# Inverting the 32x32 diagonal blocks of a gated delta rule as two 16x16 halves per block

## The chip, the cores and the metric

The kernel runs on one core of one Trainium2 chip. The metric is device time in microseconds for one execution. Three runs of the kernel before gave 2830.55, 2837.04 and 2839.18 us, so the median is 2837.04 us.

## The reference, cut to what matters

The kernel is one block of a hybrid model: a modulated norm, a mixer that has an RG-LRU branch and a gated delta-rule branch (8 heads of 128, two directions), an output projection, and a feed-forward part with squared ReLU. The data is 512 latent tokens and 256 context tokens, everything in float32. The change touches the delta rule alone, which works in chunks and solves one unit triangular system for each:

```
l_mat = jnp.einsum('bhncd,bhnsd->bhncs', k_beta, k_c) * decay
rhs = jnp.concatenate([v_beta, k_beta * jnp.exp(g_cum)[..., None]], axis=-1)
sol = lax.linalg.triangular_solve(l_mat, rhs, left_side=True, lower=True, unit_diagonal=True)
u_c, w_c = sol[..., :dv], sol[..., dv:]
qk = jnp.einsum('bhncd,bhnsd->bhncs', q_c, k_c) * decay
...
v_new = u_i - jnp.einsum('bhck,bhkv->bhcv', w_i, state)
o_i = jnp.einsum('bhck,bhkv->bhcv', q_dec_i, state) + jnp.einsum('bhcs,bhsv->bhcv', qk_i, v_new)
state = state * cd_i[..., None, None] + jnp.einsum('bhck,bhcv->bhkv', k_dec_i, v_new)
```

## The kernel before, in words

The kernel works in chunks of 128 tokens, twice the reference's. For each chunk it forms the inverse of the unit triangular 128x128 matrix explicitly, and then multiplies by it.

**Stages.** First come the modulation vectors (to about 165 us). Then `run_tiles` (L485) works through a hand-written order `ORD` (L1164) of output columns of the input projection; each tile multiplies 16 pieces of weights, split in a high and a low part, with the tokens (L498 to L500, three products each). `project` (L1334) then does the output projection, and `ff1_half`, `ff1` and `ff2` the feed-forward part. The first matrix of a weight piece is cast on ScalarE (L67), the low part is a subtraction on VectorE or GpSimd (L61). L61 and L64 are the lines of the helpers `tt` and `stt`, so that many different operations carry them; the tile names tell these apart.

**Order of the work.** Everything beside the tiles is a generator. `slot()` (L388) is called once for each piece of a tile (12 matmuls of 512 columns, or 24 of 256) and gives every generator a turn: it adds 2.8 us of VectorE and 2.2 us of ScalarE to a budget, and a generator runs on to its next `yield v, a, wait` as long as both budgets are positive; `v` and `a` are costs written by hand, and `wait` is a number of slots to stand back. `boundary()` (L430) fixes how far an instruction may be moved from the slot in which it was written: three slots on TensorE, SyncE and GpSimd, two on ScalarE, one on VectorE. So the weight matmuls of a tile and the work of the delta rule lie in one queue on each engine, in an order that is fixed when the kernel is built.

**The delta rule.** `Group.run` (L804) runs six times: two groups of context heads and four of latent heads. It builds the matrices `Ab` for both directions (L814 to L857), 16 of 128x128 in all, so that there are 64 diagonal blocks of 32x32. `Cm` (L868 to L872) collects these. Two VectorE transposes (L880) bring each block whole into two lanes (partitions) as `L`. A lane holds every second row of the inverse in the PSUM bank `Wt`, starting from the unit matrix (L885 to L888). Then 31 steps (L890 to L897), each a product (`tmp`) and a subtraction (`Wt`), finish the inverse; every fourth step ends in a `yield 1.4, 0, 0`. Two transposes (L901, L902) bring the result back as `YT` and `Yc`. The 32x32 inverses are then joined to 64x64 (products L925, L934, L937) and to 128x128 (L948 to L958), and the recurrence over the chunks follows (L977 to L1049). `afree` counts the groups that may hold `Ab` (2, later 3) and those that may hold `L` (1).

Small products in this part are given as 32x32 tiles: contraction over 32 partitions, output into 32 partitions of a PSUM bank. One of these float32 matmuls leaves two records in the trace. PSUM has 8 banks, which `bank()` hands out in turn to tiles, evacuations and the delta rule alike.

Of the kernel before, what the change touches and what calls it, by code (L numbers as in the profile page):

```python
# [7 lines left out]
F32 = mybir.dt.float32  # L8
F32R = mybir.dt.float32r
I32 = mybir.dt.int32  # L10
AF = mybir.ActivationFunctionType
ALU = mybir.AluOpType
# [4 lines left out]
P = 128  # L17
# [14 lines left out]
def build(tc, A, out, stop=None, dump=None):  # L32
    nc = tc.nc
    V, S, G, T, SP = nc.vector, nc.scalar, nc.gpsimd, nc.tensor, nc.sync
    es = ExitStack()
    with es:
        cp = es.enter_context(tc.tile_pool(name="const", bufs=1))
        wp = es.enter_context(tc.tile_pool(name="weights", bufs=2))
        pp = es.enter_context(tc.tile_pool(name="pages", bufs=29))
        ld_n = 5  # L40

        pg = ps = es.enter_context(tc.tile_pool(name="psum", bufs=8, space=PSUM))
# [3 lines left out]
        def nm(s):  # L46
            cnt[0] += 1
            return f"{s}_{cnt[0]}"

        def page(dt=F32, tag="pg", shape=(P, 512), bufs=None):  # L50
            kw = {} if bufs is None else {"bufs": bufs}
            return pp.tile(list(shape), dt, tag=tag, name=nm(tag), **kw)

        def bank(pool=None, tag="b"):
            return (pool or ps).tile([P, 512], F32, tag=tag, name=nm("bk"))

        def const(shape, dt, name):
            return cp.tile(list(shape), dt, name=name, tag=name)

        def tt(e, out, a, b, op):  # L60
            e.tensor_tensor(out=out, in0=a, in1=b, op=op)  # L61

        def stt(out, a, s, b, op0, op1):
            V.scalar_tensor_tensor(out=out, in0=a, scalar=s, in1=b, op0=op0, op1=op1)  # L64
# [7 lines left out]
        ones = const([P, P], F32, "ones")  # L72
# [33 lines left out]
        def quad(nm_, dt=F32R):  # L106
            return pp.tile([P, 4, 512], dt, tag="q8", name=nm(nm_), bufs=8)
# [31 lines left out]
        for src, n, dst in ((v1, 128, c1), (v2, 121, c2), (v3, 96, c3)):  # L139
            b = bank()  # L140
# [24 lines left out]
        def rsqrt(x, w):  # L165

            y = sm.tile([P, 16], I32, tag="rq_y", name=nm("rqy"))[:, :w]
            t = sm.tile([P, 16], F32, tag="rq_t", name=nm("rqt"))[:, :w]
            V.tensor_scalar(out=y, in0=x.bitcast(I32), scalar1=-0.5, scalar2=MAGIC, op0=ALU.mult, op1=ALU.add)
            yf = y.bitcast(F32)  # L170
            for _ in range(3):
                stt(t, yf, -0.5, yf, ALU.mult, ALU.mult)
                tt(V, t, t, x, ALU.mult)
                stt(yf, t, 1.5, yf, ALU.add, ALU.mult)
            return yf
# [56 lines left out]
        def v4(t):  # L232
            return t.rearrange("p (u i) -> p u i", i=P)

        def transp(src):
            b = bank()
            for i in range(4):
                T.transpose(b[:, i * P:(i + 1) * P], src[:, i * P:(i + 1) * P], ident)
            return b
# [31 lines left out]

        scol = const([P, 2, 16], F32, "scol")
        shc = const([P, 2, 16], F32, "shc")
        A_BUFS = 7

        def hctx(f):

            if f < 3:
                return [page(F32R, shape=(P, 2, 256)) for _ in range(2)]
            x = pp.tile([P, 4, 256], F32R, tag="A", name=nm("Hc"), bufs=A_BUFS)  # L280
            return [x[:, 0:2], x[:, 2:4]]
# [26 lines left out]
        for j, (f, kind, k0) in enumerate(mpieces):  # L308
            if k0 == 0:
                pm = bank(pg)  # L310
            r = mraw.pop(j)
            h, l = quad("mh"), quad("ml")
# [37 lines left out]
        mpar = const([P, 2], F32, "mpar")  # L350
# [32 lines left out]
        def spawn(gen, order, rate=None, prio=0):  # L383
            t = Task(gen, order, rate, prio)
            tasks.append(t)
            return t
# [27 lines left out]
        def finish(t):  # L414
            while not t.done:
                t.step()
            for l in (tasks, evacs):
                if t in l:
                    l.remove(t)
# [241 lines left out]
        def gates(n, res):  # L661
# [3 lines left out]
            def evac(pt):  # L665
# [4 lines left out]
                for t in range(NT):  # L670
                    T.transpose(b[:, t * 32:(t + 1) * 32], gf[:32, t * P:(t + 1) * P], ident[:32, :32])
                key = "L" if n == LAT else "C"
                raw = page(shape=(P, 32, NT))
# [69 lines left out]
        class Group:  # L743
# [60 lines left out]
            def run(self):  # L804
# [8 lines left out]
                afree[0] -= 1  # L813
                Ab = [pp.tile([P, 8, P], F32, tag="A", name=nm("A"), bufs=A_BUFS) for _ in range(2)]  # L814
                if lat:
                    ptD = dp.tile([2, 2, P, 512], F32, tag="ptD", name=nm("ptD"), bufs=3)
                sh4 = [P, 4, P]
                for p in range(2):
                    rr, dts = [], []
                    for d in range(2):  # L820
# [3 lines left out]
                        for u in range(4):  # L824
                            S.activation(v4(rh)[:, u, :], mk, AF.Copy, scale=gt["gh"][:, o + u:o + u + 1].bitcast(F32))
                            G.tensor_scalar(out=v4(rl)[:, u, :], in0=mk, scalar1=gt["gl"][:, o + u:o + u + 1].bitcast(F32),
                                            scalar2=0.0, op0=ALU.mult, op1=ALU.add)
# [40 lines left out]
                Cm = page(shape=(P, 16, 32))  # L868
                for b in range(4):
                    sb = slice(32 * b, 32 * b + 32)  # L870
                    S.copy(Cm[sb, 0:8], blk(Ab[0], b, 32 * b, 32))
                    V.transpose(Cm[sb, 8:16], blk(Ab[1], b, 32 * b, 32))  # L872
                yield 1.4, 1.3, 0
                while not afree[1]:
                    yield 0, 0, H0
                afree[1] -= 1
                L = pp.tile([P, 32, 32], F32, tag="A", name=nm("L"), bufs=A_BUFS)
                cv_ = Cm.rearrange("p u i -> p i u").unsqueeze(2).to_broadcast([P, 32, 2, 16])
                for i in range(2):
                    V.transpose(L[:, 16 * i:16 * i + 16].rearrange("p i (e j) -> p i e j", e=2), cv_[:, 16 * i:16 * i + 16])  # L880
                Lr = L.rearrange("p i j -> p j i")
                wf = bank()
                Wt = wf.rearrange("p (j i) -> p j i", i=32)
                tmp = page(shape=(P, 16, 32))
                V.memset(wf, 0.0)  # L885
                for e in range(2):
                    V.tensor_scalar(out=wf[:, e:512:34], in0=ones[:, 0:16], scalar1=mpar[:, e:e + 1], scalar2=0.0,
                                    op0=ALU.mult, op1=ALU.add)  # L888
                yield 1.6, 0, 0
                for l in range(31):  # L890
                    nr = l // 2 + 1
                    sh = [P, nr, 31 - l]
                    tt(V, tmp[:, :nr, l + 1:], Wt[:, :nr, l:l + 1].to_broadcast(sh), Lr[:, l:l + 1, l + 1:].to_broadcast(sh),
                       ALU.mult)
                    tt(V, Wt[:, :nr, l + 1:], Wt[:, :nr, l + 1:], tmp[:, :nr, l + 1:], ALU.subtract)
                    if l % 4 == 3:
                        yield 1.4, 0, 0  # L897
                afree[1] += 1
                Yc = page(shape=(P, 16, 32))
                YT = page(shape=(P, 16, 32))  # L900
                V.transpose(YT.rearrange("p u (r e) -> p r e u", e=2), Wt.rearrange("p r (e u) -> p r e u", e=2))  # L901
                V.transpose(Yc, YT)  # L902
                yield 1.9, 0, 0
                Ud = (Yc[:, 0:8], YT[:, 8:16])
                Dd = (YT[:, 0:8], Yc[:, 8:16])

# [15 lines left out]
                for u in range(8):  # L922
                    for d in range(2):
                        for i, j in pairs(d):
                            T.matmul(bP[sl32(j), u, :], Ab[d][sl32(i), u, sl32(j)], Dd[d][sl32(i), u, :],  # L925
                                     start=True, stop=True)
# [4 lines left out]
                for u in range(8):  # L931
                    for d in range(2):
                        for i, j in pairs(d):
                            T.matmul(bU[d][sl32(i), u, :], Pn[sl32(j), u, :], Ud[d][sl32(j), u, :],  # L934
                                     start=True, stop=True)
                            if (d, j) in ((0, 1), (1, 2)):
                                T.matmul(bU[d][sl32(j), u, :], Ud[d][sl32(j), u, :], Pn[sl32(j), u, :],  # L937
                                         start=True, stop=True)
# [38 lines left out]
                for st in range(1 if lat else 2):  # L977
                    sv = v4(Sst[h0 // 2 + st])
                    for s in range(NT):
                        ch = []  # L980
                        for d in range(2):
                            for hh in range(2):
                                p = hh if lat else st
                                t = s if d == 0 else NT - 1 - s
                                u = t if lat else hh * 2 + t
# [24 lines left out]
                        bY = v4(bank())  # L1010
# [49 lines left out]
                r = rsqrt(ss, 8)  # L1060
# [10 lines left out]
                for p in range(2):  # L1071
                    b = transp(O[p])
# [93 lines left out]
        H0, H1, H2, H3 = 1, 1, 1, 1  # L1166
        PG = (2, 2, 2, 2, 2, 2)
        PL = (-1, -1, -3, 1, -3, -1, -1, -1)
        PU, PO, NA, FILL = -1, (-1, -2, 1), 3, 0.0
        afree = [2, 1]  # L1170

        def T_(col, n, ev, m=P):
            return dict(col=col, m=m, n=n, hl=hl_lat if n == LAT else hl_ctx, evac=ev)
# [6 lines left out]
        def mods(chunks, after=None):  # L1180
            for ch in chunks:
                for f in range(4):
                    yield from modacc(ch, f, after)
# [3 lines left out]
        def set_rate(r):  # L1187
            if modtask:
                modtask[0].rate = r or None
# [4 lines left out]
        def set_lru(n):  # L1194
            LRU_MAX[0] = n
# [8 lines left out]
            "F": [lambda: finish(lh)], "m": [lambda: modtask.append(spawn(mods((2, 3, 4)), 3, MOD_RATE or None, PO[1]))],  # L1204
            "L": [lambda: set_lru(2)],
            "1": [lambda: set_rate(0)], "2": [lambda: set_rate(0.6)],
# [13 lines left out]
        for d in seq:  # L1220
            if not callable(d):
                e = (V, G) if d["n"] == CTX else (G, G)
# [20 lines left out]
        def big4(i):  # L1243
            if i < 3:
                xs = [pp.tile([P, 1024], F32, tag="A", name=nm("big"), bufs=A_BUFS) for _ in range(2)]
                return [xs[c // 2][:, c % 2 * 512:c % 2 * 512 + 512] for c in range(4)]
# [254 lines left out]
        b = NB - 1  # L1501
        wl_ = []
        for c in range(4):
            h8, l8 = quad("w2h"), quad("w2l")
            for k0 in range(0, 4, 2):
                r = wp.tile([P, 1024], F32, tag="wr", name=nm("wr"), bufs=3)
# [38 lines left out]
```

## Time and profile before

| what | value |
|---|---|
| median of three runs | 2837.04 us |
| profiled execution, its own time | 2838.08 us |
| its span, first to last instruction | 2836.3 us |
| mean granted TensorE clock | 0.970 |
| the six inversions, first transpose of `L` to last transpose back (start of L880 to end of L902) | 296.2 to 328.2, 476.1 to 539.1, 640.2 to 685.5, 758.4 to 823.9, 1049.2 to 1098.9, 1150.5 to 1194.4 us |

In the page and the views of the profile, PE is TensorE, PEld its weight loads, DVE VectorE, ACT ScalarE, POOL GpSimd. Rows of groups end in the busy time, the mean length of one in ns, and the engine's idle time just before them with what ended it. Rows of waits give total us, times, and the longest. Rows of stretches give from:to, length, the busy time of each engine with its number of instructions, and then the granted clock, the share of time in which the DMA engines were busy, and GB/s.

### The profile page before, as it was taken

The page shows a single profiled execution, that of the slowest core. Times are in us where ns is not written, and L with a number is a line of the kernel's source. Part 1 is how long each engine was busy: PE and PEld are TensorE (multiplying, and loading weights), DVE is VectorE, ACT ScalarE, POOL GpSimd, SP SyncE. Part 2 cuts the span into 40 slices and gives each one's busy share as a digit, 9 for nine tenths or more (in the row PEclk, how much of TensorE's full clock was granted, in tenths as well). Part 3 has the DMA queues.
Part 4 walks back from the last instruction along what each step waited for, and adds up shares of the span by engine and source line. Part 5 has one row for each costly group of instructions (what it writes and reads, how often), then busy time and mean ns, then how long its engine had stood idle before and what let it go on. Part 6 is the DMA issues. An engine that isn't in the chain of part 4 may idle for free.

```text
span 2836.3 us, 39412 instructions
## 1 busy us (share of the span) xinstructions
PE 2652.2 (94%) x14189; PEld 2187.4 (77%) x14189; DVE 1694.6 (60%) x3286; ACT 1193.2 (42%) x2374; POOL 639.1 (23%) x580
## 2 busy tenths in 40 slices
PE   5788899899999998977999999999999999999998
PEld 1278797788777887766898887888888888888886
DVE  6787757777696777836598533443434444334436
ACT  4546466654556564535553222222222222222222
POOL 3545344344344353315410000000000000000002
PEclk8899999999999998988999999999999999999999
DMA  7854465466566666746678433333333333333335
GB/s 269 269 141 140 109 179 170 145 188 192 172 178 194 190 199 210 223 153 202 203 259 280 160 99 115 97 97 97 97 97 97 97 97 98 96 99 97 98 98 155
DMA packets 376629, 436.39 MB, mean 154 GB/s; under 512 B 22793, under 2 KB 213602, under 8 KB 376434
## 3 DMA queue, kind: packets, MB, share of 16 engines
q1 hardware_dynamic: 376434, 433.89, 49.2%
q8 instruction: 111, 1.82, 0.3%
q14 instruction: 84, 0.69, 0.1%
HBM read 402.35 MB, written 31.46 MB: 153 GB/s over the span
## 4 chain that ended last, share of the span: by engine, by line
PE 57%; DVE 3%; DMA 2%; issue 1%; POOL 1%; ACT 1%; SPq 0%; DVEq 0%; ACTq 0%; POOLq 0%
PE bk L1461 8%; PE bk L1459 8%; PE bk L1460 8%; PE bk L1448 7%; PE bk L1450 7%; PE bk L1449 7%; PE bk L1370 2%; PE bk L1371 2%; PE bk L1369 2%; PE bk L1420 1%; PE bk L1419 1%; PE bk L1418 1%; DVE pg L61 1%; DMA wr<-in_w_ff 1%; PE bk L498 1%
## 5 line engine op out<-in xcount | busy, mean ns | idle before, releaser
L67 ACT CAST wh<-wr 128x512 fp32r<-128x512 f32 x952 | 584.6, 618 | 1226.9 <-PE bk L1449 446.1
L61 DVE TENSOR_TENSOR wl<-wr,wh 128x512 fp32r<-128x512 f32 x642 | 462.9, 723 | 785.8 <-ACT wh L67 664.6
L61 POOL TENSOR_TENSOR wl<-wr,wh 128x512 fp32r<-128x512 f32 (+1 forms) x310 | 403.8, 1308 | 594.5 <-ACT wh L67 537.2
L1461 PE MATMUL bk<-wl,pg 128*128 128x512 f32 x960 | 373.7, 389 | 0.0
L1459 PE MATMUL bk<-wh,pg 128*128 128x512 f32 x960 | 373.7, 389 | 0.0
L1460 PE MATMUL bk<-wh,pg 128*128 128x512 f32 x960 | 373.6, 389 | 0.0
L1448 PE MATMUL bk<-H2h,wh 128*128 128x512 f32 x896 | 350.0, 391 | 0.0
L1449 PE MATMUL bk<-H2l,wh 128*128 128x512 f32 x896 | 349.2, 390 | 0.0
L1450 PE MATMUL bk<-H2h,wl 128*128 128x512 f32 x896 | 349.2, 390 | 0.0
L498 PE MATMUL bk<-Hlh,wh 128*128 128x512 f32 (+1 forms) x784 | 318.5, 406 | 0.0
L500 PE MATMUL bk<-Hlh,wl 128*128 128x512 f32 (+1 forms) x784 | 311.5, 397 | 1.8 <-POOL wl L61 1.8
L499 PE MATMUL bk<-Hll,wh 128*128 128x512 f32 (+1 forms) x784 | 311.8, 398 | 0.0
L61 POOL TENSOR_TENSOR big<-big,pg 128x512 f32<-128x512 f32 x9 | 12.2, 1369 | 1248.0 <-ACT pg L1521 1248.0
L1461 PEld LDWEIGHTS bk<-wl,pg 128*128 128x128 f32 x960 | 180.3, 188 | 37.6 <-DVE wl L61 0.4
L1460 PEld LDWEIGHTS bk<-wh,pg 128*128 128x128 f32 x960 | 180.3, 188 | 37.4
L1459 PEld LDWEIGHTS bk<-wh,pg 128*128 128x128 f32 x960 | 180.3, 188 | 37.2
L1449 PEld LDWEIGHTS bk<-H2l,wh 128*128 128x128 f32 x896 | 168.7, 188 | 35.4 <-issue 0.4
L1448 PEld LDWEIGHTS bk<-H2h,wh 128*128 128x128 f32 x896 | 168.5, 188 | 35.1 <-issue 0.2
L1450 PEld LDWEIGHTS bk<-H2h,wl 128*128 128x128 f32 x896 | 168.6, 188 | 35.0
L500 PEld LDWEIGHTS bk<-Hlh,wl 128*128 128x128 f32 (+1 forms) x784 | 149.5, 191 | 36.2 <-POOL wl L61 2.3
L498 PEld LDWEIGHTS bk<-Hlh,wh 128*128 128x128 f32 (+1 forms) x784 | 150.0, 191 | 31.0 <-ACT pg L1045 0.2
L499 PEld LDWEIGHTS bk<-Hll,wh 128*128 128x128 f32 (+1 forms) x784 | 150.0, 191 | 30.4
(336 smaller groups left out, 4577.8 us busy)
## 6 DMA issues: line engine op xcount, KB each, us to landing
wr<-in_w_ff SPq DMA_DIRECT2D x272, 512.0 KB
wr<-in_w_in SPq DMA_DIRECT2D x144, 512.0 KB
ld<-in_w_mod SPq DMA_DIRECT2D x256, 256.0 KB
mr<-in_w_mod SPq DMA_DIRECT2D x32, 1024.0 KB
wr<-in_w_out SPq DMA_DIRECT2D x64, 512.0 KB
pg<-vkD SPq DMA_DIRECT2D x88, 128.0 KB
ld<-in_x SPq DMA_DIRECT2D x32, 256.0 KB
vkD<-pg SPq DMA_DIRECT2D x24, 256.0 KB
```

The lines of the kernel that those rows point to most:

```text
L61: e.tensor_tensor(out=out, in0=a, in1=b, op=op)
L67: S.copy(hi, src)
L498: T.matmul(pt[:m, :n], wh, a, start=k == 0, stop=False)
L499: T.matmul(pt[:m, :n], wh, b, start=False, stop=False)
L500: T.matmul(pt[:m, :n], wl, a, start=False, stop=k == 15)
L1369: T.matmul(bk[t], mh[:, s_], h, start=st, stop=False)
L1448: T.matmul(bk[c], w[kk][0][:, s_], hh, start=k == 0, stop=False)
L1449: T.matmul(bk[c], w[kk][0][:, s_], hl_, start=False, stop=False)
L1450: T.matmul(bk[c], w[kk][1][:, s_], hh, start=False, stop=k == 15)
L1459: T.matmul(o, ah, h, start=k == 0, stop=False)
L1460: T.matmul(o, al, h, start=False, stop=False)
L1461: T.matmul(o, ah, l, start=False, stop=k == 3)
```

## The change

Each 32x32 block is split into its two 16x16 diagonal halves and the 16x16 quarter off the diagonal. A lane now holds one half (`mpar` is 1 in the lanes of one half and 0 in the others, and picks which), so that the 64 blocks still fill 128 lanes. 15 steps invert the halves. The halves go back, as a 32x32 matrix `Y0` with an empty quarter (and its transpose `YT0`), and the quarter follows from two products for each block: Z = -(N times YT0), with N the quarter (`Nm`), and then Z with Y0, once for the inverse and once for its transpose. `YT0` is laid out so that the first product can take N as it stands.

By engine, for each of the six groups: VectorE loses 32 of 62 step instructions, one transpose, and one of two diagonal writes, and its bank memset is half as wide; it gains one multiply-add over 256 columns and two additions over 512. ScalarE gains five copies (two over 256 columns from SBUF, two over 256 from PSUM, one over 512 from PSUM). GpSimd gains a memset. TensorE gains 64 and then 128 matmuls of 32x32x32. Three more banks are taken in turn. `L` is now an ordinary page, so that the count for it in `afree` falls away; there are 31 pages instead of 29, and 6 buffers of the tag "A" instead of 7. The costs in the `yield`s, from `Lx` to the point where the 64x64 join starts, were 13.3 us of VectorE (1.6, seven times 1.4, 1.9) and are 11.4 us of VectorE (1.8, three times 2.1, 1.9, 1.4) and 2.5 us of ScalarE, with one wait of a slot (`H1`) before the first product and none between the first and the second product.

```diff
-        pp = es.enter_context(tc.tile_pool(name="pages", bufs=29))
+        pp = es.enter_context(tc.tile_pool(name="pages", bufs=31))
...
-        A_BUFS = 7
+        A_BUFS = 6
...
-                while not afree[1]:
-                    yield 0, 0, H0
-                afree[1] -= 1
-                L = pp.tile([P, 32, 32], F32, tag="A", name=nm("L"), bufs=A_BUFS)
-                cv_ = Cm.rearrange("p u i -> p i u").unsqueeze(2).to_broadcast([P, 32, 2, 16])
-                for i in range(2):
-                    V.transpose(L[:, 16 * i:16 * i + 16].rearrange("p i (e j) -> p i e j", e=2), cv_[:, 16 * i:16 * i + 16])
+
+                Lx = page(shape=(P, 16, 32))
+                V.transpose(Lx.rearrange("p i (e j) -> p i e j", e=2), Cm.rearrange("p u (e i) -> p i e u", e=2))
+                L = page(shape=(P, 16, 16))
+                S.activation(L, Lx[:, :, 0:16], AF.Copy, scale=mpar[:, 0:1])
+                stt(L, Lx[:, :, 16:32], mpar[:, 1:2], L, ALU.mult, ALU.add)
+                Nm = page(shape=(P, 16, 32))
+                G.memset(Nm, 0.0)
+                S.activation(Nm[:, :, 16:32], Cm[:, :, 16:32], AF.Copy, scale=mpar[:, 0:1])
                 Lr = L.rearrange("p i j -> p j i")
-                wf = bank()
-                Wt = wf.rearrange("p (j i) -> p j i", i=32)
-                tmp = page(shape=(P, 16, 32))
+                wf = bank()[:, 0:256]
+                Wt = wf.rearrange("p (j i) -> p j i", i=16)
+                tmp = page(shape=(P, 16, 16))
                 V.memset(wf, 0.0)
-                for e in range(2):
-                    V.tensor_scalar(out=wf[:, e:512:34], in0=ones[:, 0:16], scalar1=mpar[:, e:e + 1], scalar2=0.0,
-                                    op0=ALU.mult, op1=ALU.add)
-                yield 1.6, 0, 0
-                for l in range(31):
-                    nr = l // 2 + 1
-                    sh = [P, nr, 31 - l]
-                    tt(V, tmp[:, :nr, l + 1:], Wt[:, :nr, l:l + 1].to_broadcast(sh), Lr[:, l:l + 1, l + 1:].to_broadcast(sh),
-                       ALU.mult)
-                    tt(V, Wt[:, :nr, l + 1:], Wt[:, :nr, l + 1:], tmp[:, :nr, l + 1:], ALU.subtract)
-                    if l % 4 == 3:
-                        yield 1.4, 0, 0
-                afree[1] += 1
-                Yc = page(shape=(P, 16, 32))
-                YT = page(shape=(P, 16, 32))
-                V.transpose(YT.rearrange("p u (r e) -> p r e u", e=2), Wt.rearrange("p r (e u) -> p r e u", e=2))
-                V.transpose(Yc, YT)
-                yield 1.9, 0, 0
+                V.tensor_copy(wf[:, 0:256:17], ones[:, 0:16])
+                yield 1.8, 0.9, 0
+                for l in range(15):
+                    sh = [P, l + 1, 15 - l]
+                    tt(V, tmp[:, :l + 1, l + 1:], Wt[:, :l + 1, l:l + 1].to_broadcast(sh),
+                       Lr[:, l:l + 1, l + 1:].to_broadcast(sh), ALU.mult)
+                    tt(V, Wt[:, :l + 1, l + 1:], Wt[:, :l + 1, l + 1:], tmp[:, :l + 1, l + 1:], ALU.subtract)
+                    if l % 5 == 4:
+                        yield 2.1, 0, 0
+                We = page(shape=(P, 16, 32))
+                for e in range(2):
+                    S.activation(We[:, :, 16 * e:16 * e + 16], Wt, AF.Copy, scale=mpar[:, e:e + 1])
+                Y0 = page(shape=(P, 16, 32))
+                YT0 = page(shape=(P, 16, 32))
+                V.transpose(YT0.rearrange("p u (e r) -> p r e u", e=2), We.rearrange("p r (e u) -> p r e u", e=2))
+                V.transpose(Y0, YT0)
+                del We, wf, Wt, tmp, L, Lr, Lx
+                yield 1.9, 0.9, H1
+                bZ = bank().rearrange("p (u i) -> p u i", i=32)
+                for u in range(16):
+                    for b in range(4):
+                        sb = slice(32 * b, 32 * b + 32)
+                        T.matmul(bZ[sb, u, :], Nm[sb, u, :], YT0[sb, u, :], start=True, stop=True)
+                Z = page(shape=(P, 16, 32))
+                S.activation(Z, bZ, AF.Copy, scale=-1.0)
+                yield 0, 0.7, 0
+                bY = [bank().rearrange("p (u i) -> p u i", i=32) for _ in range(2)]
+                for u in range(16):
+                    for b in range(4):
+                        sb = slice(32 * b, 32 * b + 32)
+                        T.matmul(bY[0][sb, u, :], Z[sb, u, :], Y0[sb, u, :], start=True, stop=True)
+                        T.matmul(bY[1][sb, u, :], Y0[sb, u, :], Z[sb, u, :], start=True, stop=True)
+                Yc, YT = Y0, YT0
+                tt(V, Yc, Yc, bY[0], ALU.add)
+                tt(V, YT, YT, bY[1], ALU.add)
+                del Nm, Z, bZ, bY, Y0, YT0
+                yield 1.4, 0, 0
...
-        afree = [2, 1]
+        afree = [2]
```

## The prediction

> **What bounds the kernel now.** I read the page first, then busy times by stage, then the same for the stretches in which an inversion runs, then what TensorE waited for, then the groups of instructions that the change touches.
>
> ```profile
> PE 2652.2 (94%) x14189; PEld 2187.4 (77%) x14189; DVE 1694.6 (60%) x3286; ACT 1193.2 (42%) x2374; POOL 639.1 (23%) x580
> ```
>
> TensorE is busy for 94% of the span, and VectorE is next. The delta rule and the tiles that it shares the queues with lie between 165 and 1268 us:
>
> ```profile
> 165.00:1130.00 965.00, 892.78 (x5796) 763.31 (x5797) 712.97 (x1538) 550.53 (x1219) 422.69 (x408) 0.96 0.59 174
> 1130.00:1268.00 138.00, 115.72 (x853) 97.69 (x854) 90.24 (x260) 59.95 (x156) 36.11 (x29) 0.93 0.62 193
> ```
>
> In these 1103 us TensorE is idle for 72.2 + 22.3 = 94.5 us. Only this idle time can be won, and any matmul that is added there is paid in full unless it falls into it. Now the six stretches around the inversions, with their sum:
>
> ```profile
> 291.00:336.00 45.00, 37.15 (x379) 28.78 (x377) 39.70 (x107) 19.35 (x43) 14.87 (x15) 0.95 0.43 112
> 468.00:550.00 82.00, 65.82 (x352) 53.99 (x351) 65.25 (x152) 46.19 (x102) 31.09 (x27) 0.92 0.49 142
> 640.00:687.00 47.00, 44.81 (x288) 37.76 (x287) 41.43 (x113) 20.30 (x54) 17.14 (x14) 1.00 0.64 197
> 755.00:861.00 106.00, 95.43 (x535) 79.93 (x534) 97.27 (x216) 53.49 (x127) 41.16 (x35) 0.98 0.58 170
> 1049.00:1104.00 55.00, 45.62 (x256) 37.12 (x255) 47.48 (x112) 26.20 (x45) 22.43 (x18) 0.91 0.71 218
> 1150.00:1202.00 52.00, 49.24 (x329) 40.80 (x328) 47.23 (x145) 27.12 (x69) 17.63 (x14) 1.00 0.69 218
> sum 387.00, PE 338.07 PEld 278.38 DVE 338.37 ACT 192.66 POOL 144.31; mean PE 56.34 PEld 46.40 DVE 56.40 ACT 32.11 POOL 24.05
> ```
>
> Here VectorE is busy for 338.4 of 387 us, 87%, and TensorE idle for 48.9 us, 12.6%. In the other 716 us VectorE has 713.0 + 90.2 - 338.4 = 464.8 us of work, 65%, and TensorE stands for 45.6 us, 6.4%. The granted clock costs something too: time by lost share is 45 x 0.05 + 82 x 0.08 + 106 x 0.02 + 55 x 0.09 = 15.9 us, and it is lowest where the waits are longest. What TensorE waited for from 165 to 1268:
>
> ```profile
> PE bk L238 <- DVE pg L64: 18.3, 6, 5.6
> PE bk L925 <- DVE pg L901: 12.0, 4, 9.4
> PE bk L238 <- DVE pg L61: 11.0, 3, 6.3
> ```
>
> The long waits end on VectorE: transposes of evacuated tiles (L238), and the first product behind an inversion (L925), with one wait of 9.4. So in these stretches TensorE and VectorE are nearly level, and VectorE's queue is what holds TensorE up.
>
> **The change, part by part: VectorE.** The steps of before and the operations to compare with:
>
> ```profile
> L61 DVE TENSOR_TENSOR pg<-bk,L 128x126 f32<-128x126 f32 (+22 forms) x186 | 58.8, 316 | 4.5
> L61 DVE TENSOR_TENSOR bk<-bk,pg 128x126 f32<-128x126 f32 (+22 forms) x186 | 48.4, 260 | 5.0
> ```
>
> ```profile
> L61 DVE TENSOR_TENSOR pg<-bk,rqy 128x512 f32<-128x512 f32 x20 | 13.3, 684 | 0.2
> ...
> L880 DVE STREAM_TRANSPOSE L<-pg 128x512 f32<-128x512 f32 x12 | 12.8, 1094 | 0.0
> ...
> L64 DVE SCALAR_TENSOR_TENSOR pg<-bk,c,pg 128x254 f32<-128x254 f32 x24 | 11.4, 474 | 11.1 <-ACT pg L530 7.4 <-ACT pg L773 3.7
> ...
> L61 DVE TENSOR_TENSOR pg<-bk,L 128x56 f32<-128x56 f32 x12 | 3.0, 250 | 0.3
> ...
> L885 DVE MEMSET bk<- 128x512 f32 x6 | 2.9, 485 | 6.0 <-ACT pg L733 5.5
> ...
> L61 DVE TENSOR_TENSOR bk<-bk,pg 128x56 f32<-128x56 f32 x12 | 2.7, 224 | 0.3
> ...
> L61 DVE TENSOR_TENSOR bk<-bk,pg 128x16 f32<-128x16 f32 x6 | 1.1, 186 | 0.2
> L61 DVE TENSOR_TENSOR pg<-bk,L 128x16 f32<-128x16 f32 x6 | 1.1, 185 | 0.2
> ```
>
> A group has 31 steps now, 31 x (316 + 260) ns = 17.9 us. The new step l works on (l+1) x (15-l) elements, 680 over 15 steps, 45 on average. Between the rows of 16 and 56 elements a product of 45 takes 233 ns and a subtraction 214, so 15 steps take 6.7 us (5.6 if all were of 16 elements, 7.1 if all of 56). The steps save 11.2 us. Beside them two transposes of 1.094, a memset of 0.485 and two diagonal writes (16 elements, priced as a step of 16, 0.19) go, 3.1 us; a transpose of 1.09, a multiply-add of 0.47, half a memset (0.24 to 0.49), one diagonal write and two additions of 0.68 come, 3.4 us. The two transposes back stay. Net 10.8 us per group, 65 us over six.
>
> That work leaves the stretches: (338.4 - 65)/387 is 71% busy. Against it stand two new hand-overs to ScalarE and back (`L` behind `Lx`, the transposes behind `We`). No row shows these; they lie between nothing, if other VectorE work is put between, and some 2 us, above which they would be longer than most of VectorE's waits for ScalarE. The mean of the nearest row, 46.0/30 = 1.5 us, gives 18 us in six groups, so that VectorE would be taken for 75%:
>
> ```profile
> DVE wl L61 <- ACT wh L67: 46.0, 30, 4.2
> ```
>
> That is nearer to the 65% of the rest than to 87%, so I take it that TensorE's idle share falls to the rest's 6.4%: 387 x 0.064 = 24.8 us, a gain of 24.1 us. Linear between the two pairs (65% with 6.4%, 87% with 12.6%) it would be 9.2%, a gain of 13; if nothing but hand-overs were left, all of 48.9. Half of the 15.9 us of clock goes with it, 8 us (0 to 15.9).
>
> **TensorE.** 64 + 128 matmuls of 32x32x32 in each group, 1152 in all:
>
> ```profile
> L925 PE MATMUL bk<-pg,A 32*32 32x32 f32 x384 | 6.2, 202 | 13.1 <-DVE pg L901 12.0 <-DVE pg L902 1.0
> L937 PE MATMUL bk<-pg,pg 32*32 32x32 f32 x192 | 6.2, 205 | 0.0
> L934 PE MATMUL bk<-pg,pg 32*32 32x32 f32 x384 | 6.2, 204 | 0.6 <-ACT pg L928 0.6
> ```
>
> A single one takes about 0.2 us, but they overlap. L934 and L937 run interleaved in the same 6.2 us: 576 records, 288 matmuls, 21.5 ns each. L925 has 192 matmuls in 6.2 us, 32 ns each, in bursts that waits have cut. So 1152 cost 24.8 to 37 us. I take 24.8, since the new loops are as dense as L934 and L937. They stand in TensorE's queue among weight matmuls that have no slack of their own, so that nothing hides them.
>
> The Trainium skill, page "TensorEngine Tiling (Array Packing)", section "Gotcha 1: PSUM Pressure", speaks against this: tiles that differ in their rows are to write to different PSUM banks and cannot use one at the same time. In the new loops all four write to one bank. By it they would run one after another (the price is with the rivals). This trace doesn't agree: L925 writes one bank from four row tiles too, and 60 of its records end within 0.72 us:
>
> ```profile
> 328.59 0.72 PE L925 MATMUL bk<-pg,A 32*32 32x32 f32 x60
> ...
> 331.13 0.21 PE L934 MATMUL bk<-pg,pg 32*32 32x32 f32 x1 [0.55 <-ACT pg L928]
> ```
>
> **The new waits.** The chain is now transposes, Z, its evacuation on ScalarE, Y, two additions on VectorE, L925. Z comes a slot or more behind the transposes and should find them done. Between Z and Y there is no wait written, so they follow each other in TensorE's queue, unless weight matmuls are moved between. The rows above show such a hand-over: 1.8 us from the last L925 (329.3) by way of L928 to L934 (331.1), with 0.55 us of it idle, since weight matmuls ran between. So 0.1 us (0.6 over six) to 1.8 us for each group, and never below nothing, as a wait gives no time back; I take 1.0, 6 us in all. Behind a TensorE that stands there, queue the weight matmuls of the next tile, and behind those ScalarE's casts that wait for free weight buffers. The wait of L925 for the transposes turns into one for the additions; it stays within the idle share above.
>
> ScalarE gains, by the rows of L928 (256 columns) and L951 (512), 4 x 0.39 + 0.60 = 2.2 us per group, 13 us on an engine that is 50% busy in the stretches:
>
> ```profile
> L951 ACT ACTIVATE pg<-bk 128x512 f32<-128x512 f32 x6 | 3.6, 595 | 3.2 <-PE bk L949 3.2
> ...
> L928 ACT ACTIVATE pg<-bk 128x256 f32<-128x256 f32 x6 | 2.3, 386 | 0.1
> ```
>
> Hidden by that slack, as is GpSimd's memset; without it they would lengthen the hand-overs counted above. The written costs fall by 1.9 us of VectorE per group, two thirds of a slot, and the new `H1` gives it back, so I move nothing at the end of the last group. The counter for `L` never held a group up, as the inversions don't overlap. Pages, "A" buffers and the three banks I cost at nothing: pages are added, and the banks turn over in a few us each. If a bank came late, TensorE would wait as it does for an evacuation, and I leave that in the range.
>
> **The sum.** 24.8 (matmuls) + 6 (Z to Y) - 24.1 (idle) - 8 (clock) = -1.3 us, against the profiled execution's 2838.1 (1.8 above its span, 1.0 above the median of the runs): 2837. The bounds of the parts added up in full reach from -40 to +35; the forecast's own part of them is about 2823 to 2854, since idle time and clock go together and the dense price of the matmuls is the nearest row.
>
> **The rivals.**
> - *VectorE was the bound, and its relief is worth all of it.* The idle time in the stretches goes entirely, and the clock returns to 1.00: -48.9 - 15.9 + 24.8 + 6 = -34, 2804; halfway to it, 2820. For it speaks that nearly all long waits name VectorE; against it, that TensorE stands for 6.4% outside the stretches too.
> - *The hand-overs take the place of the waits* (slower). Z, Y and L925 stand behind one another, and TensorE waits 1.8 us for Z's evacuation and 2 us for the two additions (2 x 0.68 and the way there and back) in each group. It decides when less than those 1.8 us of weight matmuls come between. +24.8 + 22.8 - 32.1 = +15.5, 2854; with the idle time won back only by the linear rule (13 + 4), +30.6, 2869. For it: L925 follows L901 today with nothing written between, and waited 13.1 us in all. Against: L934 behind L928 waited 0.6 us in all.
> - *The small matmuls don't overlap* and take 0.204 us each: 1152 x 0.204 = 235 in place of 24.8, about 3047. The change then wouldn't do what it says. L925 and L934 speak against it. That is also the Trainium skill's rule above.
>
> **How the numbers follow.** 0.3% of this kernel, 8.5 us, is about what a measurement can tell from no change. Forecast 0.52, of which 0.12 is faster than that, 0.29 within it, 0.11 slower; VectorE's relief 0.26; hand-overs 0.20; no overlap 0.02. So faster 0.38, same 0.29, slower 0.33. The range leaves out the far end of each rival: 2808 to 2862.
>
> **What would show it.** The steps, 15 of each kind per group at 233 and 214 ns, about 6.7 us per group. Two new groups of 32x32 matmuls near 21.5 ns each. VectorE some 65 us less busy, ScalarE 13 more. TensorE's idle time around the inversions near 25 us, and its wait for VectorE before L925 well below 13. Wrong would be: TensorE waiting for the evacuation of Z by over 1.8 us a group, the new matmuls above 32 ns, or long waits of L238 as before with VectorE at 71%.

## The result, and the profile after

The changed kernel takes 2853.94 us (median of four runs, 2850.31 to 2857.42) against 2835.88 us before on the same chip: a ratio of 1.0065, with a 95% interval of 1.0045 to 1.0086. It is 18 us slower. The forecast was 2837 within 2808 to 2862, which is no change; the time lies in the range, but the loss was not forecast. The rival of the hand-overs had named 2854, and, as will be seen, for another reason than the one that held. Executions whose mean granted clock was below 0.90 (one of four of e7 below, and one of before in the same set) are left out of the medians.

Its profiled execution took 2850.31 us, with a span of 2848.6. The first lines of its page and the instruction queue's:

```profile
span 2848.6 us, 43884 instructions
...
PE 2673.4 (94%) x16493; PEld 2203.8 (77%) x16493; DVE 1640.0 (58%) x3100; ACT 1208.3 (42%) x2406; POOL 636.4 (22%) x586
...
q8 instruction: 129, 2.11, 0.3%
```

VectorE is busy for 54.6 us less, ScalarE for 15 more, and TensorE for 21 more. TensorE has 2304 more matmul records and as many weight loads: 1152 matmuls of two records each. The last line counts the transfers (packets, MB) that bring instructions; before, it was this:

```profile
q8 instruction: 111, 1.82, 0.3%
```

There are 18 more packets, three for each of the six groups. The stretches around the inversions are shorter for VectorE (these are the same six, from before `Lx` to behind L946, which is L925's new line):

```profile
291.00:335.00 44.00, 35.38 (x665) 29.49 (x664) 25.15 (x67) 18.88 (x42) 12.44 (x15) 0.84 0.37 97
...
sum 380.00, PE 334.95 PEld 276.30 DVE 256.13 ACT 191.49 POOL 137.00; mean PE 55.83 PEld 46.05 DVE 42.69 ACT 31.91 POOL 22.83
```

VectorE is down from 87% to 67%, even below the 71 to 75% of the forecast. Not all of that is the relief: in these stretches it does 82 us less (338.4 to 256.1), over the whole span only 54.6, so some other work now lies outside them. But TensorE still stands for 45 of 380 us, and the clock in the first stretch is 0.84. The waits, from 165 us to the end of the delta rule, tell what it stands for now:

```profile
PE bk L919 <- issue: 16.6, 8, 3.7
PE bk L238 <- DVE pg L64: 10.3, 6, 3.8
PE bk L238 <- DVE pg L61: 9.4, 4, 6.3
...
PE bk L918 <- issue: 5.2, 3, 2.3
...
PE bk L918 <- ACT pg L912: 3.8, 2, 3.1
PE bk L910 <- DVE pg L61: 3.4, 1, 3.4
...
PE bk L946 <- DVE pg L61: 1.4, 1, 1.4
...
PE bk L946 <- issue: 0.2, 1, 0.2
```

The wait of L925 for VectorE, 13 us before, is 1.4 us now, and the two rows of L238 are down from 29.3 to 19.7. In their place stands a wait that TensorE did not have in the kernel before: "issue", 21.8 us in eleven places inside Y (L918 and L919), and 0.2 us right behind a Y (L946). The label means that the profile shows nothing that was waited for. The groups of small matmuls show that Z is free of it:

```profile
L919 PE MATMUL bk<-pg,pg 32*32 32x32 f32 x768 | 19.5, 203 | 16.6 <-issue 16.6
L918 PE MATMUL bk<-pg,pg 32*32 32x32 f32 x768 | 19.3, 208 | 9.0 <-issue 5.2 <-ACT pg L912 3.8
L910 PE MATMUL bk<-pg,pg 32*32 32x32 f32 x768 | 8.3, 200 | 3.4 <-DVE pg L61 3.4
```

Z (L910) has 384 matmuls in 8.3 us, 21.6 ns each. Y's 768, interleaved, take nearly the same while they run, 19.5/768 = 25 ns, but with their stalls 54 ns. One Y, cut where it stands still (columns as before, the number behind the busy time counts records):

```profile
1086.15:1087.40 1.25, 1.17 (x95) 1.01 (x95) 1.00 (x1) 0.00 (x0) 0.59 (x2) 1.00 0.30 106
1087.40:1089.05 1.65, 0.00 (x0) 0.00 (x0) 0.00 (x0) 0.00 (x0) 0.00 (x0) 1.00 0.89 240
1089.05:1090.60 1.55, 1.43 (x128) 1.32 (x128) 0.00 (x0) 0.00 (x0) 0.00 (x0) 1.00 0.32 92
1090.60:1092.50 1.90, 0.00 (x0) 0.00 (x0) 0.00 (x0) 0.00 (x0) 0.00 (x0) 0.90 0.00 0
1092.50:1093.15 0.65, 0.59 (x34) 0.56 (x33) 0.00 (x0) 0.00 (x0) 0.00 (x0) 0.50 0.00 0
```

Between the two stalls lie exactly 128 matmul records and 128 weight loads, 256 instructions. That is one packet: 4608 more instructions came in 18 more packets, and the 0.29 MB make 64 bytes an instruction and 16 KB a packet. (The kernel before fits: its 14189 matmul records and as many loads, at 64 bytes, are its 1.82 MB.) TensorE, VectorE, ScalarE and GpSimd all stand still in these two gaps. The restart after the first stall and the one after the second are 3.46 us apart (1089.10 and 1092.56, each with "issue" beside it):

```profile
1089.10 0.18 PE L919 MATMUL bk<-pg,pg 32*32 32x32 f32 x1 [1.78 <-issue]
...
1092.56 0.21 PE L919 MATMUL bk<-pg,pg 32*32 32x32 f32 x1 [2.03 <-issue]
```

The record of the transfers shows the two packets themselves. They start at 1086.62 and 1090.16 us and take 1.0 and 0.9 us, and TensorE runs again 2.48 and 2.40 us after their starts. All twelve stalls are like this: two in each group, exactly 128 matmul records apart, each ending 2.35 to 2.71 us after the start of a packet; the next packet starts only 1.0 to 2.6 us after TensorE runs again. In the second gap shown, the DMA engines are idle (0.00), so that one is not held up by the transfers of the weights.

The last row of stretches shows the granted clock at 0.50 behind the second gap, so that what follows a stall can be slow too: behind five of the six Ys the clock is at 0.50, for 3.4 to 10.2 us.

### The profile page after: what moved, and what is told of

Same layout as the page of the kernel before. It is cut to its first block, busy times and chain, and to the rows that moved or that the text cites. A ratio compares the mean times of both kernels' runs of the same rounds, so it can differ in the third digit from the quotient of the medians.

```text
span 2848.6 us, 43884 instructions
## 1 busy us (share of the span) xinstructions
PE 2673.4 (94%) x16493; PEld 2203.8 (77%) x16493; DVE 1640.0 (58%) x3100; ACT 1208.3 (42%) x2406; POOL 636.4 (22%) x586
## 4 chain that ended last, share of the span: by engine, by line
PE 78%; DVE 5%; DMA 3%; issue 2%; POOL 2%; ACT 1%; SPq 0%; DVEq 0%; POOLq 0%; ACTq 0%
PE bk L1482 8%; PE bk L1480 8%; PE bk L1481 8%; PE bk L1469 7%; PE bk L1470 7%; PE bk L1471 7%; PE bk L498 6%; PE bk L500 6%; PE bk L499 6%; PE bk L1391 2%; PE bk L1392 2%; PE bk L1390 2%; DMA ld<-in_w_mod 1%; PE bk L238 1%; DVE pg L64 1%
```

## The experiments

**Theory 1: instruction supply.** TensorE runs through 256 instructions of small matmuls in about 1.4 us, and the next 256 start only some 3.5 us after the last began. A burst that is longer than what is at hand pays for the transfer. VectorE's relief is worth what was forecast. **Theory 2: hand-overs.** The matmuls cost 21.5 ns each and the rest of the loss lies in the waits between TensorE, ScalarE and VectorE. **Theory 3:** VectorE's relief is worth nothing. Every time below is a median beside the kernel before on the same chip, which gave 2834.2 to 2835.0 us in these sets.

**e1: without the products.** Z, Y, the evacuation of Z and the two additions are left out, so that the quarter off the diagonal stays empty in the result.

```diff
-                bZ = bank().rearrange("p (u i) -> p u i", i=32)
...
-                tt(V, Yc, Yc, bY[0], ALU.add)
-                tt(V, YT, YT, bY[1], ALU.add)
```

> The changed kernel without its two products, the evacuation of Z and the two additions (the quarter off the diagonal stays empty, so this part of the inverse is left out): what is left is VectorE's relief. Theory 1 (the products cost what their bursts last, 1.3 + 6.9 us per group, because TensorE runs out of instructions in the long one, and the relief is worth what was forecast, some 32 us): 2854 - 49 - 7 = about 2798, 2790 to 2812. Theory 2 (the bursts cost 25 us and the hand-overs to ScalarE and VectorE about 9): about 2820. Theory 3 (VectorE's relief is worth nothing, and the matmuls cost the 18 us that the time rose by): about 2836.

2800.56 us, ratio 0.9889 (0.987 to 0.9907): 34.5 us faster than before, inside theory 1's 2790 to 2812. Theory 3 falls, and theory 2's 2820 does too. With each kernel measured against its own runs of before (18.1 us slower, 34.5 us faster), the products and what hangs on them cost 52.5 us. The stretch from 165 us to the last matmul of the delta rule, in the kernel before, in e1 and in the changed kernel, shows where the time goes:

```profile
165.00:1252.00 1087.00, 1005.50 (x6638) 858.91 (x6638) 796.76 (x1776) 607.28 (x1360) 457.24 (x435) 0.96 0.60 178
...
165.00:1214.00 1049.00, 989.36 (x6638) 846.90 (x6638) 738.03 (x1581) 617.80 (x1386) 457.66 (x441) 0.98 0.62 184
...
165.00:1265.00 1100.00, 1023.24 (x8942) 873.60 (x8942) 742.62 (x1593) 622.33 (x1393) 458.57 (x442) 0.97 0.59 176
```

From before to e1 TensorE's idle time falls from 81.5 to 59.6 us, by 22, and the same 6638 matmul records take 16 us less, with the granted clock at 0.98 instead of 0.96. From e1 to the changed kernel 51 us come back, 17 of them idle and 34 busy. Around the six inversions alone, cut from before `Lx` to behind the first join, e1 has VectorE busy for 75% of 283 us and TensorE idle for 19.2 us, 6.8% (6.4% was taken).

**e2: the burst alone.** The kernel before, with 64 and 128 small matmuls behind its last transpose, read by nobody.

```diff
                 V.transpose(Yc, YT)
                 yield 1.9, 0, 0
+                bZ = bank().rearrange("p (u i) -> p u i", i=32)
...
+                        T.matmul(bZ[sb, u, :], Yc[sb, u, :], YT[sb, u, :], start=True, stop=True)
...
+                        T.matmul(bY[0][sb, u, :], YT[sb, u, :], Yc[sb, u, :], start=True, stop=True)
+                        T.matmul(bY[1][sb, u, :], Yc[sb, u, :], YT[sb, u, :], start=True, stop=True)
```

> The kernel before, with the 192 small matmuls added behind its last transpose and read by nobody; no ScalarE or VectorE work is added or removed. Theory 1: the long burst stands still about twice for 2 us per group with nothing released, as in the changed kernel: 6 x 8.2 = 49 us dearer, less what VectorE catches up meanwhile (up to the 13 us of L925's waits): 2870 to 2885. Theory 2: 1152 x 21.5 ns = 25 us, 2861 at most.

2897.38 us, ratio 1.023 (1.021 to 1.0249): 62.4 us dearer, beyond even theory 1's bound. The stalls are there without any evacuation or addition (L914 and L913 are its Y, L937 the L925 that follows it):

```profile
PE bk L914 <- issue: 18.3, 8, 3.2
PE bk L908 <- DVE pg L902: 14.2, 6, 9.5
...
PE bk L937 <- issue: 8.9, 5, 2.3
...
PE bk L913 <- issue: 8.9, 4, 2.6
```

They add up to 36.1 us, because the products that follow run out as well. With the forecast's 24.8 us for the matmuls themselves that is 60.9 of the 62.4 us. The wait for VectorE in front of the burst stays (14.2 us, 13.1 before), so nothing is caught up there. The agreement is not exact bookkeeping: the mean clock falls too, from 0.970 to 0.962, and other waits change.

**e7: the same matmuls strewn.** As e2, but with 24 to 28 matmuls at each of the seven yields of the step loop.

```diff
                     if l % 4 == 3:
+                        bZ = bank().rearrange("p (u i) -> p u i", i=32)
+                        for u in range(7 if l < 23 else 6 if l < 27 else 7):
+                            for b in range(4):
+                                sb = slice(32 * b, 32 * b + 32)
+                                T.matmul(bZ[sb, u, :], Cm[sb, u, :], Cm[sb, u + 8, :], start=True, stop=True)
+                        del bZ
                         yield 1.4, 0, 0
```

> The kernel before with the same 192 small matmuls per group as e2, but strewn over the seven yields of the step loop, 24 to 28 at a time, and read by nobody. Theory 1 (instruction supply): so few at a time never empty the buffers, no stalls for nothing visible, and each matmul costs its 21.5 ns: 2835 + 25 = 2860, less what VectorE catches up (some 10): 2850 to 2860. A constant price per matmul (e2's 62 us over 1152, 54 ns): 2897 again.

2851.74 us (median of three), ratio 1.0059 (1.0042 to 1.0076): 17 us for 1152 matmuls, 15 ns each, within theory 1's 2850 to 2860. As many small matmuls cost 62 us in a burst and 17 us strewn. The place differs too, since these don't stand behind the transposes as e2's do; e8 has e2's place.

**e8: the same columns in a quarter of the instructions.** As e2, with 48 matmuls of 128 columns per group.

```diff
+                bY = [bank().rearrange("p (u i) -> p u i", i=32) for _ in range(3)]
+                for k in range(3):
+                    for u in range(0, 16, 4):
+                        for b in range(4):
+                            sb = slice(32 * b, 32 * b + 32)
+                            T.matmul(bY[k][sb, u:u + 4, :], Yc[sb, u + k, :], YT[sb, u:u + 4, :], start=True, stop=True)
+                del bY
```

> The kernel before with a burst at e2's place that streams the same columns through the same 32x32 tiles with a quarter of the instructions: 48 matmuls of 32x32x128 per group in place of 192 of 32x32x32, read by nobody. Theory 1: 96 records come before the buffers are empty, so there is no stall; array time is about 48 x 0.22/4 = 2.7 us per group if four row tiles overlap: 2835 + 16 = 2851 or less. If the array or the one PSUM bank were the limit, it would cost what e2 cost: 2897.

2842.5 us, ratio 1.0024 (1.0014 to 1.0035): 8 us, within theory 1's "2851 or less". Its small matmuls wait for VectorE only, and not once for instructions:

```profile
L909 PE MATMUL bk<-pg,pg 32*32 32x128 f32 x576 | 18.9, 288 | 15.2 <-DVE pg L902 15.2
```

So four row tiles writing one bank, with the columns of e2 and at its place, don't cost what e2 cost. With e7 this leaves the number of instructions in a short time as the limit.

**e3: a slot between Z and Y.**

```diff
-                yield 0, 0.7, 0
+                yield 0, 0.7, H1
```

> The changed kernel with a wait of one slot written between Z and Y, so that weight matmuls lie between them. Theory 1: the wait for Z's evacuation goes (3.8 us), and the long burst starts with full instruction buffers, so that one of its two stalls goes in most groups: 2854 - 4 - 10 = 2840, with stalls for nothing visible still there in Y. Theory 2: only the hand-over goes: 2850 or the same as the changed kernel.

2869.09 us, ratio 1.0126 (1.0107 to 1.0145): 34 us slower than before, 16 us worse than the changed kernel, a miss for both theories. The stalls did go down, from 22.0 to about 14 us, and the wait for Z's evacuation went, but other waits rose (evacuated tiles, casts):

```profile
PE bk L238 <- DVE pg L64: 16.1, 8, 3.5
PE bk L918 <- issue: 12.5, 6, 3.0
PE bk L238 <- DVE pg L61: 11.8, 5, 6.3
...
PE bk L498 <- ACT wh L67: 8.7, 6, 3.2
```

So this written wait has a price of its own; the runs e5, e9, e10 and e11 look at it.

**e4: half of Y by a transpose.** The transposed quarter isn't multiplied out; the finished inverse is transposed on VectorE.

```diff
-                        T.matmul(bY[0][sb, u, :], Z[sb, u, :], Y0[sb, u, :], start=True, stop=True)
-                        T.matmul(bY[1][sb, u, :], Y0[sb, u, :], Z[sb, u, :], start=True, stop=True)
+                        T.matmul(bY[sb, u, :], Z[sb, u, :], Y0[sb, u, :], start=True, stop=True)
...
-                tt(V, Yc, Yc, bY[0], ALU.add)
-                tt(V, YT, YT, bY[1], ALU.add)
+                tt(V, Yc, Yc, bY, ALU.add)
+                V.transpose(YT, Yc)
```

> The changed kernel with the second half of Y (64 of its 128 matmuls, the transposed quarter) and its addition replaced by a VectorE transpose of the finished inverse: 64 matmuls and one 0.68 us addition go, one transpose of about 0.71 us comes. Theory 1: Y's burst falls from 6.9 us to between 1.3 and 3.5 us per group, 20 to 34 us in all: 2820 to 2834. Theory 2: 6 x 64 x 21.5 ns = 8 us: 2846.

2830.55 us, ratio to before 0.999 (0.9979 to 1.0001): 4.5 us faster than before and 22.5 us better than the changed kernel, for 384 matmuls less, 59 ns each. At 21.5 ns it would have been 8 us (theory 2's 2846); theory 1 had 2820 to 2834. The stalls fall to 9.0 us:

```profile
L918 PE MATMUL bk<-pg,pg 32*32 32x32 f32 x768 | 9.6, 203 | 13.8 <-issue 9.0 <-ACT pg L912 4.7
```

**e5, e9, e10, e11: where the written wait stands.** e5 is e4 with a second wait, between Z and Y. e9 is e4 with the one wait moved from in front of Z to between Z and Y. e10 moves it in the same way in the changed kernel with all its products. e11 is e4 with no wait at all.

```diff
-                yield 1.9, 0.9, H1
+                yield 1.9, 0.9, 0
...
-                yield 0, 0.7, 0
+                yield 0, 0.7, H1
```

> e4 with a wait of one slot written between Z and Y. Theory 1 as first put (stalls of the instruction supply are what is left to win): the stalls of 9 us in e4 go and so does the wait for Z's evacuation: 2830 - 10 = 2820. But e3 came out 15 us dearer than the changed kernel, with fewer stalls. Theory 1a (each written wait delays a group by two slots, 5.5 us, and that is paid in later waits): 2835 to 2845, with no stalls in Y.

2839.22 us, ratio 1.0019 (1.001 to 1.0029), with only one "issue" wait of 0.5 us left: theory 1a, not the first.

> e4 with the one written wait moved from in front of Z to between Z and Y, so that a group is as long in slots as in e4. Theory 1: Z's evacuation and the instruction supply have a slot's time, Z may wait for the transposes instead (as L925 did before, 2 us per group): 2820 to 2832. Theory 1a: no delay is added, so nothing of e5's loss.

2823.17 us, ratio 0.9968 (0.9957 to 0.998): faster than both kernels. Five of six Ys have no stall inside; the last, in the output projection, has one of 4.3 us:

```profile
L918 PE MATMUL bk<-pg,pg 32*32 32x32 f32 x768 | 7.9, 193 | 4.3 <-issue 4.3
L910 PE MATMUL bk<-pg,pg 32*32 32x32 f32 x768 | 7.7, 193 | 3.4 <-DVE pg L61 3.2 <-DVE pg L902 0.2
```

> The changed kernel with all its products, and only the written wait moved from in front of Z to between Z and Y (the move of e9 without e4's transpose). Theory 1: 128 matmuls in Y (512 instructions) still empty the buffers once per group, so about one stall of 2 us stays in each Y and one goes; Z's evacuation is no longer waited for: 2854 - 10 - 4 = 2840, 2834 to 2846, between the changed kernel and e4. If it were the hand-over alone that cost: as e9 plus 8 us, 2831.

2848.76 us, ratio 1.0056 (1.0037 to 1.0075): somewhat above what theory 1 expected, and far above the 2831 that a hand-over alone would have given. The stalls stay, 512 instructions being too many at once even with a slot in front of them:

```profile
PE bk L918 <- issue: 12.2, 5, 3.5
...
PE bk L919 <- issue: 4.5, 2, 2.3
```

> e4 without any written wait around the two products (e9 without its one). Theory 1a, as the pairs e5 to e9 and e3 to e10 give it (a written wait costs 16 to 20 us): 2823 - 16 = 2807, if the stalls of the instruction supply didn't come back. Theory 1: Z (256 instructions) and Y (256) then follow each other as in e4, the stalls of about 9 us and the wait for Z's evacuation come back, and Z waits for the transposes: 2807 + 9 + 5 + 6 = 2827, so 2818 to 2830.

2827.88 us, ratio 0.9979 (0.9969 to 0.9988): within theory 1's interval, and not theory 1a's 2807. The stalls are back (8.1 us in L918). Its interval overlaps that of e9, so that the one wait between Z and Y is at best slightly better than none. The wait in front of Z, alone, makes no difference that these runs can tell (e4 is 4.5 us faster than before, e11 6.3). Beside a wait between Z and Y it costs 16 us (e5 against e9) or 20 us (e3 against e10). Why the second one costs so much, and the first next to nothing, was not settled.

## Why the prediction was wrong, point by point

- **The steps** were right: the new ones take 225 and 212 ns on average, 15 x 0.437 = 6.6 us per group against 6.7 forecast.

```profile
L61 DVE TENSOR_TENSOR pg<-bk,pg 128x15 f32<-128x15 f32 (+7 forms) x90 | 20.3, 225 | 2.1
L61 DVE TENSOR_TENSOR bk<-bk,pg 128x15 f32<-128x15 f32 (+7 forms) x90 | 19.1, 212 | 2.4
```

- **The relief of VectorE** was right in size. The operations that the change touches take 137 us before and 71 after, 66 less where 65 were forecast; the engine as a whole is only 54.6 us less busy, and where the rest went is not shown.
- **The worth of the relief** was right in sum: 24.1 + 8 = 32 us were forecast, and e1, which has the relief without the products, is 34.5 us faster than before. The choice of the 6.4% against the linear rule (17 us) was the right one. The parts fit less well. In the profiled executions the clock term is 16 us, twice what was taken. The idle term is 22 us, but not all of it lies where it was looked for: the forecast's stretches run on behind the inversions (to 861 us, where the fourth ends at 824), and cut like those of e1 the kernel before is idle there for 31.6 of 346 us, e1 for 19.2 of 283. So 12 of the 22 us come from the inversions.
- **The matmuls were the step that failed**: "I take 24.8, since the new loops are as dense as L934 and L937". They are as dense, but far longer. In each group L934 and L937 come as 48 matmuls, 192 instructions, and then end; Z and Y are 192 matmuls, 768 instructions, nearly in one piece. The price of a short burst was carried over to a long one. While it runs a matmul costs 21.6 to 25 ns as forecast, 27.8 us in all (8.3 + 19.5), but Y stands for 21.8 us more, a term that the sum does not have, and its upper bound, 37 us by the row of L925, was no bound, as L925 is a short burst too. Between e1 and the changed kernel TensorE is busy for 34 us more: the 27.8, and some 6 that go with the lower clock (0.97 for 0.98). It is idle for 17 us more, less than the stalls, since some other waits are shorter there (L238 behind L64 10.3 us, 15.7 in e1).
- **"Nothing hides them"** was too strict as well: in e7 and e8, in the kernel before with its waits, small matmuls cost less than they last (17 us where the forecast's price gives 24.8, and 8 for 18.9 us).
- **Z to Y** was put at 6 us and is 3.8. Right in size.
- **The clock** was to give back 8 us. From 165 us to the end of the delta rule its mean is 0.96 before, 0.98 in e1 and 0.97 in the changed kernel, where stretches at 0.50 follow most of the stalls. So the products take back a part of what the relief gives. The means over the whole span (0.970, 0.975, 0.970) hold stages that the change does not touch.
- **The rival of the hand-overs** gave the measured time and not its cause: of its 1.8 + 2 us per group, 22.8 in all, the trace shows 3.8 + 1.4. That its sum came out is chance.
- **Matmuls that don't overlap** did not occur: 384 matmuls of Z, from four row tiles into one bank (each into its own 32 partitions), take 8.3 us, where a single one lasts about 0.2 us. The rule of the Trainium skill, page "TensorEngine Tiling (Array Packing)", section "Gotcha 1: PSUM Pressure", that row tiles cannot use one bank at the same time, does not hold here; the measurement decides.
- The list of what would prove the prediction wrong held one sign that came true, matmuls above 32 ns, by way of the stalls (54 ns). TensorE waits for Z's evacuation for 3.8 us in all, not for over 1.8 us a group.

## What to carry to other kernels

A price per instruction that is read from a short burst holds for short bursts; before it is multiplied by a longer one, ask how many instructions the engine can be given in that time. Here about 256 every 3.5 us, so that 32x32 matmuls of two records and two loads each (64 of them in 256 instructions) cost 54 ns in a long burst, and strewn among long instructions 15 ns (e7). Cutting instructions (half of a product by a transpose on an engine that has just been relieved), with the wait where the burst can be split, turned a change that lost 18 us into one that gains 11 (e9).

## What the runs showed of the hardware that was not expected

- TensorE's instructions come in packets of 16 KB, 256 instructions. In a burst of 32x32 matmuls a packet lasts 1.4 us. TensorE goes on only 2.35 to 2.71 us after the next packet's transfer has started, though the transfer takes 0.9 to 1.3 us, and the restarts of one burst are 3.45 to 5.10 us apart. The stalls inside Y, 0.9 to 3.7 us each, are put down to "issue" by the profile.
- Matmuls of 32x32x128 in four row tiles cost 66 ns each (18.9 us for 288), against 21.6 ns for 32x32x32: four times the columns for three times the price, and with no stall.
